# Where the second MLP's table transfers run: eight in the first MLP's beginning and sixteen behind the convolution's last block sum

## The chip, the cores and the metric

The kernel runs on one core of one Trainium2 chip. Its time is the device time of one launch in microseconds; the median of three runs is given, and one more execution was profiled. PE is TensorE's matrix multiplication and PEld its loading of weights, DVE is VectorE, ACT is ScalarE, POOL is GpSimd and SP is SyncE. POOL and SP do little here but issue DMA transfers, each from its own queue in order; a transfer that has to wait for an earlier one holds up everything behind it in its queue.

## The reference, cut to what matters

One sequence of 512 tokens with 1024 features goes through two layers in float32. The first mixes by attention (eight forgetting heads, eight stick-breaking heads), the second by a gated short convolution, and behind each mixer stands a gated MLP with a causal convolution of width 3:

```
for layer in range(DEPTH):                       # DEPTH = 2
    if layer % 2 == 0:  h = h + attention_mixer(h, ...)
    else:               h = h + short_conv_mixer(h, ...)
    h = h + conv_ffn(h, ffn_norm[layer], ffn_w_up[layer], ffn_conv[layer], ffn_w_down[layer])

def short_conv_mixer(h, norm_g, w_in, conv_w, w_out):
    proj = rms_norm(h, norm_g) @ w_in            # 1024 x 3072
    gate_b, gate_c, u = split(proj)
    return (gate_b * causal_dwconv(gate_c * u, conv_w)) @ w_out

def conv_ffn(h, norm_g, w_up, conv_w, w_down):
    u = causal_dwconv(rms_norm(h, norm_g) @ w_up, conv_w)   # 1024 x 5632
    g, val = u[..., :2816], u[..., 2816:]
    return (silu(g) * val) @ w_down              # 2816 x 1024
```

## The kernel before, in words

**Stages.** In order of time: attention (to about 255 us), the first MLP (layer 0, to about 613 us), the convolution mixer (to about 790 us, its output projection included), the second MLP (layer 1, to the end). Each float32 operand is split into a high and a low part, and every product is three matmuls.

**Products with seven in place of eight.** Most of the large products are done block-wise, on blocks of two by two, by a scheme that needs seven block products in place of eight, on sums and differences of blocks. For an up-projection this is the class `Sevens`: the columns are worked in groups `g` of 256, and each group passes through seven slots `s` (`slot(g, s)`, L1126), with one block product of 24 matmuls in each: `p1`, `p7`, `p3` (of the group before), `p6`, `p2`, `q5`, `q4`. The convolution's input projection (`conv_seven`, L1304) does its first eight column blocks with ordinary products (L1414) and then groups 1 to 4 in this way, 28 slots (L1432) and three more.

**Where a group's weights come from.** Slot 0 loads `W` of the group and `X`, `Y` of the next one through SP's queue (L1144 to L1147); slot 5 loads `Z` and converts the next group's `X` into the operand of `p1` (`weights_of`, on ACT for the high part, L1003, and DVE for the low part, L1005). In the convolution the sums of weight blocks are made by accumulating DMAs from POOL's queue: `add_block(g + 1, "Y", 1, 1)` in slot 1 (L1157), and `add_block(g + 1, "X", 0, 1)` in slot 6 (in `first_sums`, L1113), behind the DVE sum `Y + X` (L1112) that must still read the old `X`. The new `X` is the operand of `q5`. These are the block sums of the title; both have the line L1082 in the profile. A tile named `X` in the program's first group stands in the trace as `Xc`, `X` or the like: `c` marks the convolution.

**Tables.** In the two MLPs two of the needed block sums per group, called "7" and "6", are made ahead, in DRAM, by POOL's queue alone (`table_steps`, L86). For layer 1 these are 24 transfers of 768 KB. There are three chunks of columns (groups 2 to 4, 5 to 7, 8 to 10), two halves of rows in each, and for a chunk and half four steps: copy a block into table 7 (L104, `t<-in_ffn_w_up`), add a block to it (L101, accumulating), copy table 7 into table 6 (L104, `t<-t`), add a block to that (L101). Each step but the first of four must wait until the one before it has landed, and POOL's queue stands still meanwhile. The steps are pinned into the program's order. I number them 0 to 23; 0 to 7 are the first chunk.

**When the table steps are issued.** `sum_far(n)` (L970) issues the next `n` steps. Before: seven behind the attention (L974), one at slots 1, 8 and 15 of the convolution (L1434), and the fourteen that are left at slot 20 (L1437). Slot 20 is slot 6 of group 3: it holds the convolution's last block sum, `X` of group 4. The second MLP reads the tables by SP's queue (`load_pair`, L1071, table 7 into `Y`; `first_sums`, L1115, table 6 into `three`): the first chunk at about 817 us, the second chunk from 868 us on, in the time of group 4, the third from 928 us on. POOL's next transfer behind the table steps is `add_block(2, "X", 0, 1)` of the second MLP's first group.

Of the kernel before, what the change touches and what calls it, by code (L numbers as in the profile page):

```python
# [46 lines left out]
FILL1, FILL2, BEFORE = 1.5, 3.3, 2.0  # L47
UNITS = (0, 1), (2,), (3,)
PLAIN = 2
FAR = 7, 1, 14  # L50
CHUNKS = (2, 3), (5, 3), (8, 3)
SHARE = 0.58

# [2 lines left out]
def trunk(  # L56
# [245 lines left out]
    def fetch(n):  # L302
        while len(ready) < min(len(wanted), at[0] + n):
            ready.append(load(len(ready)))
            split_all(len(ready) - 1)
# [664 lines left out]
    def sum_far(n):  # L970
        for _ in range(n):
            next(sums_far, None)

    sum_far(FAR[0])  # L974

# [328 lines left out]
    def conv_seven(norm, mp):  # L1304
# [126 lines left out]
        want_conv_out()  # L1431
        for s in range(28):  # L1432
            up.slot(1 + s // 7, s % 7)
            if s in (1, 8, 15):  # L1434
                sum_far(FAR[1])
            elif s == 20:
                sum_far(FAR[2])  # L1437
            if s == 27:
                fetch(1)
        for s in (0, 2, 3):  # L1440
# [198 lines left out]
    with tc.tile_pool(name="mix", bufs=1, reuse_waits="tile") as mp:  # L1639
        ys = conv_seven(norm, mp)  # L1640
        norm = Norm("n3", 8)
        hs_open(2)

        def out_products(w, acc, ks):
            for k in ks:
                y_hi, y_lo = ys[k // 4]
                mm3(acc, (w[0][:, k, :], w[1][:, k, :]), (y_hi[:, k % 4, :], y_lo[:, k % 4, :]), k == 0, k == ND - 1)

        first_two = [(weights(AHEAD - o), bank("ab"[o])) for o in range(2)]
        for w, acc in first_two:  # L1650
            out_products(w, acc, range(6))
        for o, (w, acc) in enumerate(first_two):
            out_products(w, acc, (6, 7))
            if o:
                fetch(AHEAD)
            residual_out(o, acc, norm)
        for o in range(2, ND):
            w, acc = weights(), bank("ab"[o % 2])
            out_products(w, acc, range(ND))
            residual_out(o, acc, norm)  # L1660
        norm.finish()
# [29 lines left out]
```

## Time and profile before

| what | value |
|---|---|
| median of three runs | 1132.03 us (1131.14 to 1132.06) |
| the profiled execution, its own time | 1132.23 us |
| span of the profiled execution, first to last instruction | 1130.0 us |
| granted TensorE clock, mean | 0.999 |
| PE busy | 1116.2 us of the span |
| bytes moved by DMA | 209.34 MB, 185 GB/s on average |

The page of the profile gives shares over the whole span. What a change in one stage is worth is read from narrower views: the list of who waited for whom in a window, the order of instructions of one engine, the busy time by stretches, and the time from the issue of a DMA to its landing. In a line of an engine's order the columns are start, duration, engine, line, operation, output and inputs, count, and in brackets how long the engine was idle just before and what released it.

### The profile page before, as it was taken

The page shows a single profiled execution, that of the slowest core. Times are in us where ns is not written, and L with a number is a line of the kernel's source. Part 1 is how long each engine was busy: PE and PEld are TensorE (multiplying, and loading weights), DVE is VectorE, ACT ScalarE, POOL GpSimd, SP SyncE. Part 2 cuts the span into 40 slices and gives each one's busy share as a digit, 9 for nine tenths or more (in the row PEclk, how much of TensorE's full clock was granted, in tenths as well). Part 3 has the DMA queues.
Part 4 walks back from the last instruction along what each step waited for, and adds up shares of the span by engine and source line. Part 5 has one row for each costly group of instructions (what it writes and reads, how often), then busy time and mean ns, then how long its engine had stood idle before and what let it go on. Part 6 is the DMA issues. An engine that isn't in the chain of part 4 may idle for free.

```text
span 1130.0 us, 19403 instructions
## 1 busy us (share of the span) xinstructions
PE 1116.2 (99%) x7691; PEld 1009.3 (89%) x7691; DVE 942.9 (83%) x1439; ACT 680.0 (60%) x1013; POOL 159.3 (14%) x191
## 2 busy tenths in 40 slices
PE   8999999999999999999999999999999999999998
PEld 7888787878899999999999889988889999998876
DVE  6787888887899787888979878875799888898886
ACT  7556676655466667676557345544456766677553
POOL 4011111111001110004300011111001110014300
PEclk9999999999999999999999999999999999999999
DMA  6678777777868777699953466899757766699961
GB/s 193 171 178 202 187 172 188 181 191 200 202 180 203 199 203 195 196 283 212 223 162 94 129 137 163 186 231 226 190 155 186 178 172 162 180 268 195 226 156 57
DMA packets 175690, 209.34 MB, mean 185 GB/s; under 512 B 7564, under 2 KB 140220, under 8 KB 175600
## 3 DMA queue, kind: packets, MB, share of 16 engines
q0 software_dynamic: 41024, 86.95, 38.8%
q1 hardware_dynamic: 134416, 121.09, 34.7%
q8 instruction: 60, 0.98, 0.4%
q14 instruction: 30, 0.25, 0.1%
q10 hardware_dynamic: 160, 0.07, 0.0%
HBM read 203.10 MB, written 49.28 MB: 223 GB/s over the span
## 4 chain that ended last, share of the span: by engine, by line
PE 87%; DVE 5%; DMA 3%; issue 2%; ACT 2%; DVEq 0%; ACTq 0%; POOLq 0%
PE psb L1055 25%; PE psb L1603 10%; PE psa L1055 10%; PE psa L1603 6%; PE psb L314 5%; PE psb L315 5%; PE psb L316 5%; PE psa L316 2%; PE psa L314 2%; PE psa L315 2%; DMA Xc<-in_conv_w_in 2%; PE psa L785 2%; PE psb L689 2%; DMA raw<-in_ffn_w_down 1%; DVE wlo L294 1%
## 5 line engine op out<-in xcount | busy, mean ns | idle before, releaser
L293 ACT ACTIVATE whi<-raw 128x1024 fp32r<-128x1024 f32 (+2 forms) x89 | 91.6, 1032 | 95.0 <-PE psb L315 29.7
L294 DVE TENSOR_TENSOR wlo<-raw,whi 128x1024 fp32r<-128x1024 f32 (+2 forms) x89 | 105.5, 1187 | 26.7 <-ACT whi L293 26.0
L1055 PE MATMUL psb<-p_lo,whi_p 128*128 128x256 f32 x432 | 121.6, 281 | 0.0
L1055 PE MATMUL psb<-p_hi,wlo_p 128*128 128x256 f32 x432 | 121.6, 281 | 0.0
L1055 PE MATMUL psb<-p_hi,whi_p 128*128 128x256 f32 x432 | 121.2, 281 | 0.0
L314 PE MATMUL psb<-hs_a,whi 128*128 128x512 f32 x224 | 92.2, 412 | 0.0
L316 PE MATMUL psb<-hs_a,wlo 128*128 128x512 f32 x224 | 88.7, 397 | 0.0
L1055 PEld LDWEIGHTS psb<-p_hi,whi_p 128*128 128x128 f32 x432 | 81.9, 190 | 0.0
L1055 PEld LDWEIGHTS psb<-p_lo,whi_p 128*128 128x128 f32 x432 | 81.3, 188 | 0.0
L1055 PEld LDWEIGHTS psb<-p_hi,wlo_p 128*128 128x128 f32 x432 | 81.2, 188 | 0.0
L1055 PE MATMUL psa<-p_hi,wlo_p 128*128 128x256 f32 x288 | 81.2, 282 | 0.0
L1055 PE MATMUL psb<-q_lo,whi_q 128*128 128x256 f32 x288 | 81.0, 281 | 0.0
L1055 PE MATMUL psa<-p_lo,whi_p 128*128 128x256 f32 x288 | 81.0, 281 | 0.0
L1055 PE MATMUL psb<-q_hi,wlo_q 128*128 128x256 f32 x288 | 81.0, 281 | 0.0
L1055 PE MATMUL psa<-p_hi,whi_p 128*128 128x256 f32 x288 | 80.8, 281 | 0.0
L1055 PE MATMUL psb<-q_hi,whi_q 128*128 128x256 f32 x288 | 80.8, 281 | 0.0
L1603 PE MATMUL psb<-act,whi 128*128 128x256 f32 x352 | 63.1, 282 | 0.1
L424 DVE SCALAR_TENSOR_TENSOR uv<-yv,taps,uv 128x511 f32<-128x511 f32 (+1 forms) x80 | 56.7, 747 | 0.0
L1603 PE MATMUL psb<-whi,act 128*128 128x512 f32 x176 | 56.3, 398 | 0.0
L424 DVE SCALAR_TENSOR_TENSOR ug<-yg,taps,ug 128x511 f32<-128x511 f32 (+1 forms) x80 | 55.7, 748 | 0.0
L1603 PEld LDWEIGHTS psb<-act,whi 128*128 128x128 f32 x352 | 54.2, 189 | 0.5 <-DVE act L1005 0.3
L1055 PEld LDWEIGHTS psa<-p_hi,whi_p 128*128 128x128 f32 x288 | 54.5, 189 | 0.1
(478 smaller groups left out, 3628.8 us busy)
## 6 DMA issues: line engine op xcount, KB each, us to landing
t<-in_ffn_w_up POOLq DMA_DIRECT2D x42, 768.0 KB, 8.2
t<-t POOLq DMA_DIRECT2D x18, 768.0 KB, 4.9
raw<-in_attn_w_in SPq DMA_DIRECT2D x24, 512.0 KB, 5.0
X<-in_ffn_w_up SPq DMA_DIRECT2D x18, 512.0 KB, 5.2
Y<-t SPq DMA_DIRECT2D x18, 512.0 KB, 6.1
three<-t SPq DMA_DIRECT2D x18, 512.0 KB, 3.7
W<-in_ffn_w_up SPq DMA_DIRECT2D x18, 512.0 KB, 4.0
X<-in_ffn_w_up POOLq DMA_DIRECT2D x18, 512.0 KB, 7.8
```

The costliest lines, as they stand in the source:

```text
L293: return (act.activation(hi[:, at_], raw[:, at_], AF.Copy), dve.tensor_tensor(lo[:, at_], raw[:, at_], f32(hi[:, at_]), op=ALU.subtract))
L294: dve.tensor_tensor(lo[:, at_], raw[:, at_], f32(hi[:, at_]), op=ALU.subtract))
L314: made = [pe.matmul(acc, w[0], rhs[0], start=first, stop=False), pe.matmul(acc, w[0], rhs[1], start=False, stop=False), pe.matmul(acc, w[1 ...
L315: pe.matmul(acc, w[0], rhs[1], start=False, stop=False),
L316: pe.matmul(acc, w[1], rhs[0], start=False, stop=last)]
L424: dve.scalar_tensor_tensor(dst[:, d:], src[:, 0:S - d], tap(j), dst[:, d:], op0=ALU.mult, op1=ALU.add)
L689: pe.matmul(ss[e][:, c:c + wide], ql[rows, b * P:n], kl[rows, 0:wide], start=first and b == bs[0], stop=last and b == bs[-1])
L785: pe.matmul(out_, w, t[:, first:first + step * (NB - k - 1) + 1:step, :], start=k == 0 and i == 0, stop=k == NB - 1 and i == 1)
L1055: pe.matmul(to, w[a][:, k, c], x[b][:, k, :], start=fresh and i + k + t == 0, stop=i == 1 and k == 3 and t == 2, skip_group_check=not fresh)
L1603: pe.matmul(to, l, r, start=begin and o + t == 0, stop=end and t == 2 and o == (0 if layer else 1), skip_group_check=not fresh)
```

## The change: the same 24 transfers, issued at other places

```
-FAR = 7, 1, 14
+FAR = 8, 16
@@ conv_seven
         for s in range(28):
             up.slot(1 + s // 7, s % 7)
-            if s in (1, 8, 15):
+            if s == 20:
                 sum_far(FAR[1])
-            elif s == 20:
-                sum_far(FAR[2])
             if s == 27:
                 fetch(1)
```

`sum_far(FAR[0])` behind the attention stays where it is and now issues eight steps, so that the first chunk is complete there. Steps 8 to 23, both other chunks, are issued at slot 20, behind the last block sum of the convolution. No step is added or left out, and no other instruction changes its place in the program.

## The prediction

> **What bounds the kernel now.** The page of the profile comes first, for the share of the engines.
>
> ```profile
> PE 1116.2 (99%) x7691; PEld 1009.3 (89%) x7691; DVE 942.9 (83%) x1439; ACT 680.0 (60%) x1013; POOL 159.3 (14%) x191
> ```
>
> PE is busy for 1116.2 us of a span of 1130.0 us. The change alters nothing that PE does, so it can only win or lose time in which PE stands still. Where that lies in the convolution is told by the list of what PE waited for (655 to 745 us; total, number, longest) and by the busy time in stretches (first figure the length, second PE's busy time).
>
> ```profile
> PE psa L1055 <- ACT whi_p1c L1003: 1.8, 1, 1.8
> PE psa L1055 <- DVE wlo_p1c L1005: 1.0, 2, 0.8
> PE psb L1055 <- ACT Xsc L1107: 0.6, 1, 0.6
> ```
>
> ```profile
> 660.00:683.00 23.00, 20.46 (x168) 19.90 (x168) 15.04 (x15) 11.08 (x14) 3.56 (x3) 1.00 0.77 175
> 683.00:706.00 23.00, 22.73 (x192) 22.54 (x191) 20.45 (x23) 12.97 (x16) 4.21 (x5) 1.00 0.68 172
> 706.00:726.00 20.00, 19.40 (x162) 19.02 (x161) 16.55 (x19) 10.38 (x13) 4.56 (x5) 1.00 0.72 145
> 785.00:825.00 40.00, 40.00 (x180) 32.56 (x179) 31.09 (x55) 18.12 (x26) 2.34 (x3) 1.00 0.82 205
> ```
>
> PE stands still for 23.00 − 20.46 = 2.54 us, then 0.27 us, then 0.60 us, 3.41 us in all. That is the most that this stage can give back. In the last row, where table steps run too, it is never idle. The clock is 1.00 throughout. The order of instructions of PE, ACT and SP at the largest gap shows what ends last there.
>
> ```profile
> 678.82 0.39 PE L1055 MATMUL psa<-p_hic,whi_p1c 128*128 128x256 f32 x1 [1.78 <-ACT whi_p1c L1003]
> 680.08 0.39 PE L1055 MATMUL psa<-p_hic,wlo_p1c 128*128 128x256 f32 x1 [0.76 <-DVE wlo_p1c L1005]
> ...
> 677.71 1.06 ACT L1003 ACTIVATE whi_p1c<-Xc 128x1024 fp32r<-128x1024 f32 x1 [5.72 <-DMA Xc<-in_conv_w_in]
> ...
> 666.18 0.37 SPq L1070 DMA_DIRECT2D Xc<-in_conv_w_in  x1
> ...
> 684.78 0.37 SPq L1079 DMA_DIRECT2D Wc<-in_conv_w_in  x1
> ...
> 705.67 0.37 SPq L1079 DMA_DIRECT2D Wc<-in_conv_w_in  x1
> ```
>
> PE is through with the work before at 678.82 − 1.78 = 677.04. The next product is `p1` of group 2. Its operand is made from that group's `X`, which SP asked for at 666.18 and which had not landed until about 677.6. ACT had been free for it since 677.71 − 5.72 = 671.99. So a load that took 11.4 us is the cause of the 1.78 + 0.76 = 2.54 us.
>
> Why it took so long is seen from POOL's order beside it (first three rows; the others serve below) and from issue to landing, the last figure of a row, for loads and adds of 512 KB and the table step of 768 KB.
>
> ```profile
> 662.14 1.28 POOL L1082 DMA_DIRECT2D Xc<-in_conv_w_in  x1 [63.14 <-DVE Yc L1112]
> 662.89 1.84 POOL L1082 DMA_DIRECT2D Yc<-in_conv_w_in  x1
> 663.64 2.06 POOL L101 DMA_DIRECT2D t<-in_ffn_w_up  x1
> ...
> 724.74 1.17 POOL L104 DMA_DIRECT2D t<-t  x1
> ...
> 734.70 0.91 POOL L104 DMA_DIRECT2D t<-in_ffn_w_up  x1
> ...
> 784.06 0.90 POOL L104 DMA_DIRECT2D t<-in_ffn_w_up  x1
> ...
> 808.11 0.88 POOL L101 DMA_DIRECT2D t<-in_ffn_w_up  x1 [4.71 <-DMA t<-t]
> 831.84 1.33 POOL L1082 DMA_DIRECT2D X<-in_ffn_w_up  x1 [22.85 <-DVE wlo_p L1005]
> ```
>
> ```profile
> Yc<-in_conv_w_in POOLq DMA_DIRECT2D x1, 512.0 KB, 9.9
> t<-in_ffn_w_up POOLq DMA_DIRECT2D x1, 768.0 KB, 13.8
> Xc<-in_conv_w_in SPq DMA_DIRECT2D x1, 512.0 KB, 11.4
> Wc<-in_conv_w_in SPq DMA_DIRECT2D x1, 512.0 KB, 6.5
> Wc<-in_conv_w_in SPq DMA_DIRECT2D x1, 512.0 KB, 4.2
> ```
>
> The `Y` add of 662.89 landed at 672.8. Table step 7, issued at 663.64, landed at 677.4, and `X` at 677.6 with it. The two `Wc` rows are SP loads of the same size, issued at 684.78 and 705.67 beside two such adds; they went before most of the table step had begun and took 6.5 and 4.2 us. So adds alone do not make a load take 11.4 us; the table step behind them is what is left.
>
> **The change part by part.** (1) Step 7 leaves slot 1. The trace does not show this load without it; its landing is bounded by the `Wc` rows below (4.2 to 6.5 us) and by its own 11.4 us above. I take 6.5, the busier of the near ones. `X` then lands at 672.7, ACT converts it at once, and by the old distance from ACT's start to the low part's use (677.71 to 680.08, 2.37 us) all is ready at 675.1, ahead of 677.04. The whole 2.54 us go. They go as long as the load lands by 677.04 − 2.37 = 674.67, in 8.5 us. Next in line is `p7` of group 2, whose `Y` landed at 672.8 anyway.
>
> (2) Steps 8 and 9 leave slots 8 and 15. The add of `X` goes ahead of them in POOL's queue, so they hardly hold it. But the 0.27 and 0.60 us come from ACT and DVE being late with `q5`, whose `X` add is issued behind the sum `Y + X`, and in group 2 that sum waited for the late load. With it earlier, some of this goes too. Bounds 0 and 0.87; I take half, 0.43.
>
> (3) POOL issues the same 24 transfers as before, three of them elsewhere; the issues themselves (2.06 us in the row above) hold nothing up, since POOL has nothing else to do until the next group's slot 6. Cost 0.
>
> (4) The tail at slot 20 begins with step 8 in place of step 10 and is two steps longer. Four steps take (784.06 − 734.70) / 2 = 24.68 us by the rows of two rounds. With the convolution 2.97 us earlier, step 8 is issued at 724.74 − 2.97 = 721.8, step 20 three rounds on at 795.8, and step 23 as far behind step 20 as before (808.11 − 784.06 = 24.05) at 819.9. Queued behind it is POOL's `X` add of the second MLP's first group, at 831.84 − 2.97 = 828.9, which waits for DVE and not for the tail. When that add must land, and what else is loaded then, shows in these rows, landings first.
>
> ```profile
> t<-in_ffn_w_up POOLq DMA_DIRECT2D x1, 768.0 KB, 6.8
> X<-in_ffn_w_up POOLq DMA_DIRECT2D x1, 512.0 KB, 7.7
> raw<-in_conv_w_out SPq DMA_DIRECT2D x1, 512.0 KB, 11.8
> ...
> 817.36 0.37 SPq L1071 DMA_DIRECT2D Y<-t  x1
> ...
> 868.12 0.44 SPq L1071 DMA_DIRECT2D Y<-t  x1
> ...
> 830.00 1.04 ACT L1003 ACTIVATE whi_p<-Y 128x1024 fp32r<-128x1024 f32 x1
> 842.22 1.05 ACT L1003 ACTIVATE whi_q<-X 128x1024 fp32r<-128x1024 f32 x1
> ...
> 846.72 0.28 PE L1055 MATMUL psb<-q_hi,whi_q 128*128 128x256 f32 x1
> ```
>
> Step 23 lands 6.8 us later, at 826.7, just ahead of the add. The loads of the second MLP's first group now run beside it. If `Y`, asked for at 817.36, took even the 11.4 us of the convolution, it would land at 828.8, before ACT's 830.00. Loads during the tail are covered as well: one for the output projection took 11.8 us and PE never waited. The second chunk's tables are first read at 868.12. I cost the tail at 0; the cover is the slack named here, and the price without it is rival C.
>
> (5) Step 7 goes behind step 6 in the first MLP's beginning.
>
> ```profile
> 300.84 0.58 POOL L104 DMA_DIRECT2D t<-t  x1 [8.24 <-DMA t<-in_ffn_w_up]
> 323.73 1.35 POOL L1082 DMA_DIRECT2D X<-in_ffn_w_up  x1 [22.30 <-DVE wlo_p L1005]
> ...
> t<-t POOLq DMA_DIRECT2D x1, 768.0 KB, 4.9
> ...
> 307.78 0.37 SPq L1071 DMA_DIRECT2D Y<-t  x1
> ...
> 321.83 1.04 ACT L1003 ACTIVATE whi_p<-Y 128x1024 fp32r<-128x1024 f32 x1
> ```
>
> It is issued when step 6 has landed, at 305.7, and even in 13.8 us has landed by 319.5, with POOL's next transfer at 323.73. The nearest load, `Y` at 307.78, is wanted at 321.83, so 11.4 us would do. Cost 0.
>
> **The sum.** 1132.23 us (the profiled execution) − 2.54 − 0.43 = 1129.26, so **1129.2 us**; that execution is 0.2 us above the median of the runs, 1132.03. What a measurement of this kernel can tell from no change is 0.2%, 2.3 us, so the forecast lies little beyond it.
>
> **The rivals.**
>
> A, the forecast: 1128.6 to 1129.8. For it speaks that step 7 and `X` land together, and the shorter `Wc` loads.
>
> B, the stall stays or only moves: the `Y` add and the three SP loads that follow `X` are enough to hold it beyond 8.5 us, or a load elsewhere pays for the steps. Then between nothing and 2.2 us is won, 1129.9 to 1132.2, centre 1131.3. For it speaks that the busy share of the DMA engines is high there and in the tail (0.77 and 0.82 in the rows of stretches); against it the 4.2 and 6.5 us loads, and PE's full busy time beside the old tail.
> The Trainium skill ("DMA: Bandwidth & Descriptors", "Issuing engines are not separate DMA queues") says that transfers from all queues run on the same 16 engines and interleave; by that, the three steps take as much from their neighbours at the new place as at the old. The trace agrees as to the taking (11.8 us in the tail), but the old tail's loads have the slack that `X` in slot 0 lacks; a full return of the loss gives 1132.2.
>
> C, slower: the tail ends late and the `X` add behind it starves `q5` of the second MLP's first group. PE takes `q5` at 846.72, so by the 2.37 us above the add has to land by 844.35, 841.4 on the earlier clock. Behind another transfer it lands some 3 us after that one (an estimate from the `Y` add, issued 0.75 us behind an `X` add and landing in 9.9 us, against 7.7 us for an `X` add). So step 23 has to be issued by 841.4 − 3 − 6.8 = 831.6; it decides from 11.7 us more than forecast over four rounds, at 27.6 us a round against 24.68. With 30 us a round it is 10 us late: 1139 us. With the 13.8 us of step 7 for each step it would be far more. Against it: both rounds measured took the same, beside equally dense loads.
>
> **How the numbers follow.** A 0.60, B 0.26, C and any other lateness 0.14. Faster by over 0.2%: 0.57 from A and 0.03 from B, 0.60. Within: 0.03 from A and 0.22 from B, 0.25. Slower: 0.14 and 0.01, 0.15. The range begins at 1128.3, which is 1132.03 − 3.41 less the 0.3 us by which runs differ, and ends at 1132.7, behind all of B; C is outside.
>
> **What would show it.** In the changed profile, `X` of group 2 lands within 8.5 us, and PE's wait for `whi_p1c` and `wlo_p1c` falls from 2.8 us to below 0.5. PE's idle time from 660 to 726 is below 1 us. The last table step is issued near 820 us, POOL's next `X` add near 829 us, waiting for DVE. Part 1 is wrong if `X` still takes 10 us without step 7; part 4 if the tail's rounds take over 27 us, or if PE waits for any load between 725 and 850 us.

## The result, and the profile after

The changed kernel takes 1128.6 us (median of 8 runs) where the kernel before takes 1131.8 (8 runs), a ratio of 0.9973 with a 95% interval of 0.9962 to 0.9984. The gain is 3.2 us, by the interval 1.8 to 4.3. Run again with some of the experiments it stood at 1128.72 against 1132.58, ratio 0.9966 (0.9954 to 0.9978). The profiled execution took 1129.78 us with a span of 1127.6. One run of an experiment below (step 7 at slot 4) took 1174.54 us at a mean granted clock of 0.88, and its ratio leaves that run out.

The list of what PE waited for in the convolution, and the busy time in stretches (length, then busy time and instructions of PE, PEld, DVE, ACT, POOL, then the clock, the DMA share and GB/s), of the changed kernel:

```profile
PE psb L1055 <- ACT Xsc L1107: 0.9, 1, 0.9
PE psa L1055 <- DVE wlo_p1c L1005: 0.4, 1, 0.4
```

```profile
660.00:683.00 23.00, 23.00 (x192) 22.75 (x191) 18.59 (x19) 12.72 (x15) 5.19 (x4) 1.00 0.66 156
683.00:706.00 23.00, 22.58 (x190) 22.38 (x190) 19.74 (x21) 12.96 (x16) 2.60 (x2) 1.00 0.61 144
706.00:726.00 20.00, 19.11 (x159) 18.72 (x158) 16.23 (x19) 9.30 (x12) 1.92 (x2) 1.00 0.54 109
785.00:825.00 40.00, 40.00 (x180) 32.55 (x179) 31.09 (x56) 18.30 (x26) 4.37 (x6) 1.00 0.89 233
```

The 2.54 us of the first stretch are gone to the last hundredth; in the second and third stretch 0.42 and 0.89 us are left, where 0.27 and 0.60 had been. PE's idle time from 660 to 726 us falls from 3.41 to 1.31 us, where below 1 had been forecast. The order of PE, ACT and SP at the old gap, and the landing of `X` of group 2:

```profile
677.70 0.28 PE L1055 MATMUL psa<-p_hic,whi_p1c 128*128 128x256 f32 x1
...
674.49 1.06 ACT L1003 ACTIVATE whi_p1c<-Xc 128x1024 fp32r<-128x1024 f32 x1 [1.68 <-DMA Xc<-in_conv_w_in]
...
667.00 0.37 SPq L1070 DMA_DIRECT2D Xc<-in_conv_w_in  x1
...
Xc<-in_conv_w_in SPq DMA_DIRECT2D x1, 512.0 KB, 7.4
```

The load takes 7.4 us in place of 11.4, and PE goes from `q4` to `p1` with nothing in between. POOL's order shows the tail and what is queued behind it; below it are the landings of the last step and of the add, and the use of the add on ACT and PE.

```profile
680.34 1.29 POOL L1082 DMA_DIRECT2D Xc<-in_conv_w_in  x1 [14.78 <-DVE Yc L1112]
...
722.93 1.17 POOL L104 DMA_DIRECT2D t<-in_ffn_w_up  x1
...
748.33 0.59 POOL L104 DMA_DIRECT2D t<-in_ffn_w_up  x1
...
799.58 0.89 POOL L104 DMA_DIRECT2D t<-in_ffn_w_up  x1
...
826.15 0.87 POOL L101 DMA_DIRECT2D t<-in_ffn_w_up  x1 [6.99 <-DMA t<-t]
830.04 1.33 POOL L1082 DMA_DIRECT2D X<-in_ffn_w_up  x1 [3.02 <-DVE wlo_p L1005]
```

```profile
t<-in_ffn_w_up POOLq DMA_DIRECT2D x1, 768.0 KB, 7.1
X<-in_ffn_w_up POOLq DMA_DIRECT2D x1, 512.0 KB, 10.0
...
840.43 1.05 ACT L1003 ACTIVATE whi_q<-X 128x1024 fp32r<-128x1024 f32 x1
...
844.93 0.28 PE L1055 MATMUL psb<-q_hi,whi_q 128*128 128x256 f32 x1
```

The last step is issued 3.9 us before the add, not 9 as forecast, and the add takes 10.0 us in place of 7.7. It lands at 840.0, and ACT takes it at 840.43 without a wait.

From the profiles three lengths can be set side by side: from PE's first `p1` matmul of the convolution to the first matmul of its output projection; from there to the first block product of the second MLP; from there to the end.

| kernel | block products of the convolution, us | output projection and the second MLP's first products, us | second MLP from there, us |
|---|---|---|---|
| before | 744.14 − 659.59 = 84.55 | 90.75 | 1130.0 − 834.89 = 295.1 |
| changed | 742.36 − 660.41 = 81.95 | 90.74 | 1127.6 − 833.10 = 294.5 |
| only step 7 moved | 81.96 | 90.75 | 294.7 |
| only steps 8 and 9 moved | 84.04 | 90.74 | 294.5 |
| step 7 at slot 4 | 85.26 | 90.75 | 294.5 |
| front 10, tail 14 | 80.85 | 90.74 | 294.4 |
| tail 17 | 80.71 | 90.75 | 294.5 |
| tail 18 | 81.38 | 90.75 | 294.5 |
| tail 19 | 80.51 | 90.75 | 305.6 |
| tail 20 | 80.81 | 90.74 | 310.6 |
| later split | 80.34 | 90.75 | 294.5 |
| front 9, later split | 80.95 | 90.75 | 294.4 |
| changed, again | 81.53 | 90.75 | 294.5 |

The middle column is the same to 0.01 us, whatever runs beside it. The kernels that keep step 7 among the block sums need 84.0 to 85.3 us in the first column, all others 80.3 to 82.0. One execution of each was profiled; the two of the changed kernel lie 0.42 us apart (81.95 and 81.53), so smaller differences in this column say nothing. In the third column the two kernels with the longest tails stand out; they are taken up below.

### The profile page after: what moved, and what is told of

Read it like the earlier page. It is cut to its first block, busy times and chain, and to the rows that moved or that the text cites. A ratio compares the mean times of both kernels' runs of the same rounds, so it can differ in the third digit from the quotient of the medians.

```text
span 1127.6 us, 19408 instructions
## 1 busy us (share of the span) xinstructions
PE 1115.7 (99%) x7691; PEld 1009.9 (90%) x7691; DVE 943.0 (84%) x1439; ACT 679.7 (60%) x1013; POOL 157.7 (14%) x191
## 4 chain that ended last, share of the span: by engine, by line
PE 89%; DVE 4%; issue 2%; DMA 2%; ACT 2%; SPq 0%; DVEq 0%; ACTq 0%; POOLq 0%
PE psb L1055 25%; PE psb L1601 11%; PE psa L1055 10%; PE psa L1601 8%; PE psb L314 5%; PE psb L315 5%; PE psb L316 5%; PE psa L314 2%; PE psa L316 2%; PE psa L315 2%; PE psa L785 2%; PE psb L689 2%; DMA Xc<-in_conv_w_in 2%; PE psb L571 1%; PE psc L316 1%
## 5 line engine op out<-in xcount | busy, mean ns | idle before, releaser
L1055 PEld LDWEIGHTS psb<-q_hi,whi_q 128*128 128x128 f32 x288 | 54.6, 190 | 0.0
```

The source lines that it names most:

```text
L1055: pe.matmul(to, w[a][:, k, c], x[b][:, k, :], start=fresh and i + k + t == 0, stop=i == 1 and k == 3 and t == 2, skip_group_check=not fresh)
```

## The experiments

**Which of the three steps it was.** Only step 7 goes to the front, or only steps 8 and 9 to the tail:

```
-FAR = 7, 1, 14
+FAR = 8, 1, 14            # only step 7:      "if s in (8, 15):" in place of "(1, 8, 15)"
+FAR = 7, 1, 16            # only steps 8, 9:  "if s == 1:"       in place of "(1, 8, 15)"
```

> Step 7 alone goes to the first MLP's beginning; steps 8 and 9 stay at slots 8 and 15 of the convolution, fourteen steps at slot 20. Theory (the gain is step 7's alone, because it lands beside the load of X of group 2): X of group 2 lands in about 7.4 us, PE waits for neither whi_p1c nor wlo_p1c of group 2, and the whole of the change's gain comes, 2.4 to 3.2 us below the kernel before. Rival (each of the three steps costs its share): about a third, 1.1 us.

> Step 7 stays at slot 1 of the convolution; steps 8 and 9 go behind the last block sum, sixteen steps there. Theory (step 7 alone): X of group 2 again takes about 11 us, PE's waits of about 1.8 and 0.8 us for p1 of group 2 stay, and the time is that of the kernel before within 0.6 us. Rival (each its share): about 2.1 us faster.

Step 7 alone: 1128.59 us, ratio to the kernel before 0.997 (0.9958 to 0.9982), all of the gain; `X` of group 2 took 7.3 us. Steps 8 and 9 alone: 1132.75 us, ratio 1.0006 (0.9997 to 1.0015), none of it. PE's waits in the convolution, first with step 7 moved, then with steps 8 and 9 moved:

```profile
PE psb L1055 <- ACT Xsc L1107: 0.6, 1, 0.6
PE psa L1055 <- DVE wlo_p1c L1005: 0.4, 1, 0.4
```

```profile
PE psa L1055 <- ACT whi_p1c L1003: 0.8, 1, 0.8
PE psa L1055 <- DVE wlo_p1c L1005: 0.8, 1, 0.8
```

In the second kernel step 7 stands at slot 1 again, the load took 10.5 us, and the wait for `p1` is back. So one transfer of 24 made the whole loss, since one load beside it had no slack; the two others run beside loads that have it: SP's load of `Z` at 710.53 took 11.2 us beside step 9 and 6.4 us in the changed kernel (at 708.45), and PE waited for it in neither.

**Whether the place in the program or in the queue counts.** Step 7 goes to slot 4 (`if s in (4, 8, 15)`), behind the place where SP's load of `X` is written in the program.

> As the kernel before, but step 7 stands at slot 4 of the convolution's first group in the program in place of slot 1, behind the place where X of group 2 is loaded; steps 8 and 9 at slots 8 and 15 and fourteen at slot 20 as before. Theory (what comes before a step in POOL's queue sets its time, not its place among the other engines' work): nothing stands between slot 1 and slot 4 in that queue, so step 7 is issued within 1 us of where it was, X of group 2 takes 10 to 12 us again, PE's waits of 0.8 to 1.8 us for p1 of group 2 stay, and the time is that of the kernel before within 0.6 us. Rival (the place in the program sets the time, step 7 comes some 8 us later and misses the load): 2 to 3 us faster.

1131.9 us, ratio 1.0003 (0.9994 to 1.0011): no gain. In POOL's order the step is issued 0.75 us behind the `Y` add, just as before, since nothing between the two places stands in that queue, and `X` took 11.3 us. So the place in the queue set its time, and the place in the program did not.

```profile
664.35 2.06 POOL L101 DMA_DIRECT2D t<-in_ffn_w_up  x1
...
Xc<-in_conv_w_in SPq DMA_DIRECT2D x1, 512.0 KB, 11.3
```

The stretches of this profile just behind the gap show something that the profile of the kernel before did not:

```profile
679.00:682.00 3.00, 1.80 (x12) 1.60 (x13) 2.58 (x3) 2.28 (x3) 0.00 (x0) 0.95 0.55 178
682.00:685.00 3.00, 3.00 (x16) 3.00 (x16) 2.97 (x4) 0.01 (x1) 0.83 (x2) 0.50 0.00 1
685.00:688.00 3.00, 3.00 (x26) 3.00 (x26) 2.37 (x4) 1.56 (x3) 2.42 (x3) 0.98 0.62 82
```

From 682 to 685 us PE is busy, but at a granted clock of 0.50, and gets 16 matmuls done where the next stretches show 26 and more: about 12 matmuls at the full pace of 0.12 us each, some 1.4 us, on top of the wait. The kernel with steps 8 and 9 moved shows it too, behind a gap of only 0.84 + 0.76 us:

```profile
682.00:685.00 3.00, 3.00 (x18) 3.00 (x18) 3.00 (x4) 0.85 (x2) 1.60 (x2) 0.59 0.02 5
685.00:688.00 3.00, 3.00 (x28) 3.00 (x27) 2.44 (x3) 1.48 (x3) 1.04 (x1) 1.00 0.85 130
```

**How long the tail may be.** Seventeen to twenty steps behind the last block sum, the rest in front (`FAR = 7, 17`, `6, 18`, `5, 19`, `4, 20`), on the changed kernel:

> Seven steps at the first MLP's beginning, none among the block sums, seventeen behind the last one. Theory: as in the changed kernel the convolution's stall is gone; step 8 goes out right behind step 7, so the tail grows by only 3 to 6 us; the X add of the second MLP's first group is issued near 830 us and lands 3 to 5 us later than the 840.0 of the changed kernel, so ACT waits for it for 2 to 5 us and PE for 0 to 3 us. Time 0 to 3 us above the changed kernel. Rival (the tail still has slack): no difference to the changed kernel.

> Six steps at the first MLP's beginning, eighteen behind the last block sum: between the seventeen that cost nothing and the twenty that cost 19 us. Theory (one us per us once ACT gets the X add of the second MLP's first group later than about 841.6 us on the clock of the kernel with seventeen): the last step is issued near 832 us, the add lands near 844 us, PE waits 1 to 4 us for q5, and the time is 1 to 4 us above the changed kernel. Rival (the price comes in whole rounds or only with several late adds): within 0.6 us of it.

> Five steps at the first MLP's beginning, nineteen behind the last block sum. Theory (one us per us from the point at which ACT gets the X add of the second MLP's first group later than about 841.6 us): the last step is issued near 836 us, the add lands near 846 us, PE waits 3 to 7 us for q5, and the time is 3 to 8 us above the changed kernel. Rival (the price is a jump of some 10 us or more as soon as the add is late at all): over 10 us above it.

> Four steps at the first MLP's beginning, twenty behind the last block sum: one round of four more in the tail. Theory (past the slack a late tail costs PE one us per us through the X add queued behind it): the last step is issued near 826 + 25.5 = 852 us, the X add lands near 862 us where about 842.5 would do, and the time is 17 to 20 us above the changed kernel. Rival (the tail competes for bandwidth only, PE goes on): 0 to 3 us above it.

| steps in the tail | median, us | ratio to the kernel before (95%) | last step issued | PE's wait for `q5`, us |
|---|---|---|---|---|
| 16 (changed, again) | 1128.72 | 0.9966 (0.9954 to 0.9978) | 823.63 (826.15 in the first profile) | 0 |
| 17 | 1127.95 | 0.9965 (0.9952 to 0.9977) | 827.46 | 0 |
| 18 | 1128.67 | 0.999 (0.9968 to 1.0012) | 828.89 | 0 |
| 19 | 1139.8 | 1.0067 (1.005 to 1.0084) | 836.81 | 8.4 |
| 20 | 1147.86 | 1.0142 (1.0127 to 1.0158) | 845.04 | 13.5 |

The first row is from the later job, beside the kernel with nineteen; the other rows stand against the kernel before in their own jobs. The wait for `q5` is that of the second MLP's first group.

With seventeen the rival held, and with eighteen it did by the median (the interval of its ratio reaches past 1; two long runs are named below): the add goes out in the same breath as the last step, ACT waits for it for about 1 us, and PE has that much to spare. The rows are ACT's in the kernel with seventeen, then with eighteen:

```profile
839.07 1.06 ACT L1003 ACTIVATE whi_q<-X 128x1024 fp32r<-128x1024 f32 x1 [1.00 <-DMA X<-in_ffn_w_up]
```

```profile
839.71 1.06 ACT L1003 ACTIVATE whi_q<-X 128x1024 fp32r<-128x1024 f32 x1 [0.86 <-DMA X<-in_ffn_w_up]
```

Of the eight runs with eighteen, six lie between 1127.7 and 1129.6 us and two at 1135.7 and 1136.3. Those two were not profiled; a late add would look like that, but it is not shown, and one run of the kernel with ten steps in front, whose tail ends early, took 1136.35 us as well. With nineteen, POOL and PE read:

```profile
836.81 0.88 POOL L101 DMA_DIRECT2D t<-in_ffn_w_up  x1 [5.25 <-DMA t<-t]
837.37 1.68 POOL L1082 DMA_DIRECT2D X<-in_ffn_w_up  x1
...
850.57 0.58 PE L1055 MATMUL psb<-q_hi,whi_q 128*128 128x256 f32 x1 [8.42 <-ACT Xs L1107]
```

My 3 to 8 us were too few; the loss against the changed kernel in the same job is 1139.8 − 1128.72 = 11.1 us, so the number of the rival held. The profile says why: the wait is 8.4 us, and the second MLP is 305.6 − 294.5 = 11.1 us longer, 2.7 more than the wait. The add went out right behind the last step and took 10.9 us, so it landed at 848.3, and PE went on 2.3 us later. With twenty the wait is 13.5 us and the stage 310.6 − 294.5 = 16.1 us longer, 2.6 more. PE's row and the stretches around it in the kernel with twenty:

```profile
857.33 0.58 PE L1055 MATMUL psb<-q_hi,whi_q 128*128 128x256 f32 x1 [13.50 <-ACT Xs L1107]
...
853.00:858.00 5.00, 0.67 (x3) 0.67 (x4) 1.79 (x2) 2.88 (x4) 0.00 (x0) 0.50 0.70 111
858.00:863.00 5.00, 5.00 (x27) 5.00 (x27) 4.65 (x8) 3.10 (x6) 0.43 (x1) 0.54 0.46 127
863.00:868.00 5.00, 5.00 (x45) 5.00 (x44) 4.72 (x7) 3.21 (x5) 0.86 (x1) 1.00 1.14 279
```

When PE is released it works at half the clock for about 5 us: 27 matmuls in place of 45, which is 18 × 0.12 = 2.2 us, most of the 2.6. The median is 1147.86 − 1128.6 = 19.3 us above the changed kernel (in different jobs), inside the 17 to 20 us that I had expected, but by luck in part: the last step went out at 845.04 and not near 852, and the profile accounts for 16.1 us alone. (This profiled execution, 1144.61 us, is the fastest of its four; the others lie at 1147.35 to 1148.65, and what they lost more is not shown.)

**Whether the front is free too.** Ten steps in front, fourteen behind (`FAR = 10, 14`):

> Ten steps at the first MLP's beginning, none among the block sums, fourteen behind the last one. Theory (PE has no wait in either place, so where the steps run costs nothing as long as no late one holds an add of PE's weights): step 9 is issued near 312 us, ahead of POOL's X add at 324, the tail ends near 813 us, the X add of the second MLP's first group lands in under 8 us, and the time is that of the changed kernel within 0.6 us. Rival (the loads of the first MLP's first group suffer as X of group 2 did): 1 to 3 us above the changed kernel.

1127.96 us (the median of twelve runs, one of them at 1136.35), ratio 0.9971 (0.9957 to 0.9984): the time of the changed kernel. But POOL's order shows that the front is nearly full:

```profile
320.55 0.90 POOL L101 DMA_DIRECT2D t<-in_ffn_w_up  x1 [10.33 <-DMA t<-in_ffn_w_up]
323.74 1.36 POOL L1082 DMA_DIRECT2D X<-in_ffn_w_up  x1 [2.30 <-DVE wlo_p L1005]
```

Step 9 came 8 us later than I had expected, 3 us ahead of the first MLP's first `X` add; the add took 10.0 us, and PE waited 0.2 us for `q5` there.

**What is left in the convolution.** On the changed kernel, the split of the first two output columns is moved from slot 6 of group 2 to slot 4 of group 3, so that DVE comes to the sum `Y + X` sooner:

```
             elif s in (3, 4):
                 conv(2 * p + s - 3, u[:, s - 3, :])
+                if (p, s) == (2, 4):
+                    halves_in(0, 2)
...
-            elif s == 6 and p == 1:
-                halves_in(0, 2)
```

> The changed kernel, with the split of the convolution's first two output columns into high and low parts moved from slot 6 of group 2 to slot 4 of group 3, so that DVE comes to the sum Y + X of group 3 about 1.2 us earlier and POOL can issue that group's X add as much earlier. Theory (what is left of PE's idle time in the convolution, 0.4 and 0.9 us, comes from q5 waiting for an X add that a busy DVE releases late): the wait of PE behind Xs of group 3 falls to below 0.3 us, time 0.3 to 1 us below the changed kernel. Rival (the add's own landing time, 8 to 10 us, or the next DVE work decides): no difference to the changed kernel.

1128.17 us, ratio 0.9968 (0.9957 to 0.9978). PE waited for nothing in the convolution, and its 80.34 us are the shortest of all, but in the time this is not told from the changed kernel. Together with nine steps in front and fifteen behind:

> Nine steps at the first MLP's beginning and fifteen behind the last block sum, together with the later split of the convolution's first two output columns. Theory (both ends of the tables then have several us of slack, and PE's small waits for q5 in the convolution are gone): the last step is issued 5 to 9 us ahead of POOL's X add, PE waits less than 0.5 us between 600 and 870 us, and the time is 0 to 1.3 us below the changed kernel. Rival (the small waits were not caused by the DVE's order, or return elsewhere): no difference to the changed kernel.

1129.58 us, ratio 0.9968 (0.9957 to 0.9979), beside 0.9966 for the changed kernel in the same job, and a wait of 0.6 us behind `Xs` was back. The rival held. The last step was issued 16.6 us ahead of POOL's `X` add, not 5 to 9 as expected. These waits of 0.2 to 0.9 us stand in the profiles of most kernels here, but the kernel with steps 8 and 9 moved has none behind `Xs` either, without the split, and one execution of each cannot say that the split took them away. No version beat the changed kernel by more than can be measured.

The repeat of the changed kernel, which served as the measure for the last three kernels, was put on record with this:

> The changed kernel itself once more, beside the two below on the same chip, so that they can be set against it directly: 2.4 to 3.6 us below the kernel before.

## Why the prediction was right, point by point

The forecast of 1129.2 us against 1128.6 measured, and of 2.97 us gained on the profiled execution against 3.2 between the medians, held, and the mechanism of its main term was borne out: step 7 alone carries the gain, through the one load that it delayed. That the sum came so near is in part luck: the profiled execution gained 2.45 us (1132.23 − 1129.78), the 0.43 us of part 2 did not come, and the 3.2 us of the medians hold something that no term stood for.

**Part 1, step 7.** Right. I took 6.5 us for the load of `X` and allowed 8.5; it took 7.4, and the whole 2.54 us went.

**Part 2, steps 8 and 9.** Wrong, with its sign and in the reading behind it. I took 0.43 us from PE's small waits, and they grew from 0.87 to 1.31 us in that profile. Both waits are of group 3, and only the second is for `q5`; the first is for the low part of `p1`. PE's two rows and POOL's `X` add of that group, before and then after:

```profile
700.56 0.38 PE L1055 MATMUL psa<-p_hic,wlo_p1c 128*128 128x256 f32 x1 [0.27 <-DVE wlo_p1c L1005]
715.39 0.39 PE L1055 MATMUL psb<-q_hic,whi_q5c 128*128 128x256 f32 x1 [0.60 <-ACT Xsc L1107]
...
705.04 1.29 POOL L1082 DMA_DIRECT2D Xc<-in_conv_w_in  x1 [18.23 <-ACT psb L1153]
```

```profile
698.48 0.38 PE L1055 MATMUL psa<-p_hic,wlo_p1c 128*128 128x256 f32 x1 [0.42 <-DVE wlo_p1c L1005]
713.59 0.38 PE L1055 MATMUL psb<-q_hic,whi_q5c 128*128 128x256 f32 x1 [0.89 <-ACT Xsc L1107]
...
702.96 1.29 POOL L1082 DMA_DIRECT2D Xc<-in_conv_w_in  x1 [20.03 <-ACT psb L1153]
```

The late load of `X` held up the sum and the add of group 2. That add did go out earlier, 2.6 us behind PE's start of `p1` (677.70 to 680.34) where it had been 4.7, but PE had not waited for `q5` of group 2 before. In group 3 the add stands 4.5 us behind the first of the two rows in both kernels, so there was nothing to win there. The wait behind `Xs` varies between 0 and 0.9 us over the kernels without step 7 there; what sets it is not shown.

**Part 3, the issues.** Cost nothing, as said.

**Part 4, the tail.** Its price was right: PE waits for nothing between 725 and 870 us. In this profile its length was not: three rounds took 25.40 us (722.93 to 748.33) and 51.25 for two (to 799.58), and the last stretch 26.57 (to 826.15), not 24.68 and 24.05; so the last step came at 826.15, not 819.9, and more than half of the 11.7 us of slack that I had worked out was used. But this is scatter between executions and not a rule for longer tails, as the four profiles with sixteen steps in the tail show:

| kernel | step 8 issued | step 23 issued | between, us | landing of the `X` add, us |
|---|---|---|---|---|
| forecast | 721.8 | 819.9 | 98.1 | not given |
| changed | 722.93 | 826.15 | 103.2 | 10.0 |
| changed, again | 721.76 | 823.63 | 101.9 | 8.4 |
| later split | 722.25 | 817.94 | 95.7 | 7.3 |
| only steps 8 and 9 moved | 724.89 | 821.74 | 96.9 | 7.6 |

The forecast lies in the middle of them; what it lacked is a spread of 7.5 us. Rival C's point can be set on one clock with the runs by the second MLP's first block product, which C's clock had at 834.89 − 2.97 = 831.92: step 23 had to be issued 0.3 us before it. With eighteen steps it went out 2.5 us before (831.42 − 828.89), and that cost nothing; with nineteen 6.7 us behind (836.81 − 830.16) and with twenty 13.2 behind (845.04 − 831.84), which is 7.0 and 13.5 us past the point, and PE waited 8.4 and 13.5. So C had the point and the wait about right. Its price lacked the 2.6 or 2.7 us by which the stage grew beyond the wait.

**Part 5, the front.** Right: step 7 was issued at 302.40, landed 7.9 us later, and POOL's next transfer at 323.97 waited for DVE alone. The rows:

```profile
302.40 0.89 POOL L101 DMA_DIRECT2D t<-in_ffn_w_up  x1 [4.20 <-DMA t<-t]
323.97 1.34 POOL L1082 DMA_DIRECT2D X<-in_ffn_w_up  x1 [20.68 <-DVE wlo_p L1005]
```

**The sum.** In the two profiles the convolution's block products gained 2.60 us, of which the shorter waits are 3.41 − 1.31 = 2.10 and the rest is not accounted for. The second MLP gained 0.6, its first products 0.01, and what lies ahead of the block products lost 0.8 (660.41 − 659.59). The medians gained somewhat more, 3.2 us. The clock that may follow the old gap fits this: of the 12 runs of the kernel before that stood beside the repeat, ten had a mean clock of 0.996 to 0.999, of the changed kernel's five one had (but of its eight runs in the first job four had 0.998 or 0.999, so such a mean has other causes too). In another job, 27 runs of the kernel before split into 11 with a clock of 1.000, median 1131.35 us, and 16 below it, median 1132.26. That this is the half clock behind the gap is argued, not shown: the half clock is seen in two profiles (step 7 at slot 4, and only steps 8 and 9 moved), and the profile of the kernel before has the gap without it.

**Rival B** fell: PE waited for no load at the new place. What the Trainium skill ("DMA: Bandwidth & Descriptors", "Issuing engines are not separate DMA queues") says of transfers interleaving on the same engines is seen in the `X` add, which took 10.0 us close behind the tail against 7.7 before, but there it met slack.

## What to carry to other kernels

Here background transfers were not dear because of their bytes, but where one ran beside a load that was wanted as soon as it landed; look for such a load, and move the transfer past it in its own queue, since its place in the program did not set its time here. Before making a chain of waiting transfers longer, work out when the next transfer in that queue has to land, and leave room for the spread between executions (here 95.7 to 103.2 us for the same sixteen steps). And count a long stall of PE at more than its length (here 8.4 and 13.5 us cost 2.7 and 2.6 us on top).

## What the runs showed of the hardware that I had not expected

A gap of about 2.5 us on PE, broken by two matmuls, was followed in one execution (step 7 at slot 4) by about 3 us at a granted clock of 0.50, and in another (the profile of the kernel before) by none; with steps 8 and 9 alone moved, a gap of 1.6 us was followed by it too. Gaps of 8.4 and 13.5 us cost 2.7 and 2.6 us beyond their length. The Trainium skill ("TensorE: Matmul & The Clock Gate", "What's actually happening") states that the clock has two states, full and half, and falls to half after an idle window of about 3.4 us that runs freely, so that the effect differs from run to run. The trace agrees with the two states (0.50 and 1.00) and with the variation; from PE's first stop to steady work it was 3.04 us in the kernel before (677.04 to 680.08) and 2.9 and 2.1 us where the clock fell (677.77 to 680.70 and 677.83 to 679.93), so here stretches shorter than the page's window sufficed, and by the measurement a gap below 3 us is not safe.

The landing time of a 512 KB add by POOL goes with how far ahead of it the last table step went out. The second MLP's first `X` add took 7.3 to 7.8 us in the seven profiles where that step went out 10 us ahead or more, 8.4 and 10.0 us where it went out 5.3 and 3.9 us ahead, and 9.4 to 11.0 us in the four where it went out 0.56 us ahead.
